# Values projected one head ahead in a two-layer attention and convolution trunk

## The chip, the cores and the metric

One core of a Trainium2 chip runs the whole program. The metric is device time in microseconds (us) for one execution; the kernel before takes 2388.18 us, the median of 3 runs between 2387.6 and 2389.5.

## The reference

The input is 1024 tokens of width 1024, ahead of which 16 learned tokens are set, so L = 1040. Two layers follow. Each normalises the rows (RMS norm), multiplies by `w_in`, and splits the product into queries, keys and values of 4 heads and a 1024-wide input of a convolution branch:

```python
proj = hn @ w_in[l]
q, k, v, u = jnp.split(proj, [QK_WIDTH, 2 * QK_WIDTH, 2 * QK_WIDTH + ATTN_WIDTH], axis=-1)
...
a = p[:, :, 0] - lam * p[:, :, 1]
return jnp.einsum('bhqk,bkhe->bqhe', a.astype(v.dtype), v)
```

A head has two causal softmaxes `p`, whose difference weights the values; each head's output is normalised. The convolution branch takes the halves `a` and `gate` of `u`, forms `a * sigmoid(gate)` (a gated linear unit, GLU), convolves it with 31 taps for each channel, normalises over channels and applies SiLU. Both branches go through `w_out` and are added to the residual; then comes a SwiGLU feed-forward net of width 2816. The last step is an RMS norm.

## The kernel before, in words

Activations lie transposed, 128 channels on the partitions and the 1040 tokens along the free axis. A product in float32 is made of three matmuls of split operands, `hi*hi + hi*lo + lo*hi` (`mm3`, L272), so a weight block of 1024 by 128 costs 24 matmuls per stretch of tokens. The stretches are CH0: 272, 384 and 384 columns. Weights come by `fetch`, which takes them in the fixed order of `plan`, prepares one key ahead (AHEAD = 1), and splits each half block on ScalarE (L222) and VectorE (L223). For the input projection the keys run 0 to 19: head h has keys 3h and 3h+1 for queries and keys and 3h+2 for values; keys 12 to 19 are the four GLU blocks.

A layer's mixing stage is written in this order. The norm's column factors come from `rsqrt_cols` (matmuls L177, a power on GpSimd, L183) and are spread over the partitions by `spread` (VectorE L198, TensorE L199, ScalarE L202). The first head's queries and keys are projected by `project_qk`; in the first layer its matmuls are those of L360, which take the token blocks as they arrive and hold three `pj` buffers of PSUM until ScalarE copies them out (L368). There are just three `pj` buffers. Then, for each head h: `make_stacks` lays out queries and keys by 12 DMAs (L399); `project_v` projects this head's values (matmuls L272, copy L428, transposes L413 and L417, scaled copies L414 and L420); the head before is finalized; and `weave` runs the attention (scores L455 and L456, mask L463, softmax on VectorE and ScalarE L460 to L471, transposes L483 and L492, values L503) with a filler between its steps: the next head's `project_qk`, for the third head also the first GLU block, for the fourth head GLU blocks 1 and 2. After the fourth head come GLU block 3, `finalize` (a power on GpSimd at L535), the convolutions of blocks 2 and 3 on TensorE (`conv`, with weights that VectorE makes at L610), and the output projection of the attention half (`wout_attn`).

The convolutions of blocks 0 and 1 are done on VectorE instead (`conv_dve`): one L588 and 30 L590 for each block, each over some 1040 columns and each needing the one before, then one ScalarE copy, L592. They can start when the block's GLU is done, whose last instruction is the VectorE product of L580. They are queued in `bg`; `tick` emits one for each 2300 ns that the steps claim, and `flush` emits those left after `wout_attn(1)`. Behind them stands `conv_norm`: matmuls L636 over all four blocks, squares, another `rsqrt_cols` and `spread`, SiLU (L648) and the split that the convolution half of the output projection needs. The rest of `wout_attn`, blocks 2 to 7, is woven into `conv_norm`.

What is written sets a priority, not the final order: a scheduler places the instructions of each engine ahead of the run and may put later ones earlier where their inputs and buffers are ready. On the chip an engine then keeps that order.

Of the kernel before, what the change touches and what calls it, by code (L numbers as in the profile page):

```python
# [23 lines left out]
NH = 4  # L24
# [17 lines left out]
LA = 2  # L42

PRODS = ("a11", "s3", "s2", "s1", "a12", "a22", "s4")
OCN = (0, 4, 1, 5, 2, 6, 3, 7)
RA = 2.0
DVEJ = (0, 1)
# [34 lines left out]
def tok(i):  # L82
    return (0, META) if i == 0 else (META + P * (i - 1), META + P * i)


def build(tc, xT, w_in, w_out, w_gu, w_down, params, lams, ctab, consts, tabs, outT):
# [14 lines left out]
    def nm(s):  # L101
        uid[0] += 1
        return f"{s}{uid[0]}"

    def big(dt=F32):
        return sp.tile([P, SW], dt, tag="S", name=nm("S"), bufs=SB)
# [11 lines left out]
    def tmp(dt=F32):  # L118
        return tp.tile([P, TW], dt, tag="T", name=nm("T"), bufs=TB)
# [15 lines left out]
    def small(n=NQ):  # L135
        return tp.tile([P, 16], F32, tag="small", name=nm("s"), bufs=16)

    def ps(tag):
        return pp.tile([P, 512], F32, tag=tag, name=nm(tag), bufs=PS_BUFS[tag])
# [29 lines left out]
    def rsqrt_cols(sq, n, blocks=range(NQ)):  # L169

        i0, i1 = blocks[0], blocks[-1] + 1
        pst = ps("sc")
        ms = small()
        V.memset(ms, 1.0)
        for i in blocks:
            a, b = tok(i)
            T_.matmul(pst[:b - a, i:i + 1], lhsT=sq[:, a:b], rhs=ones[:, 0:1], start=True, stop=True)  # L177
        f0 = max(i0, 1)
        V.tensor_scalar(ms[:, f0:i1], pst[:, f0:i1], 1.0 / n, EPS, op0=ALU.mult, op1=ALU.add)
        if i0 == 0:  # L180
            V.tensor_scalar(ms[:META, 0:1], pst[:META, 0:1], 1.0 / n, EPS, op0=ALU.mult, op1=ALU.add)
        rc = small()
        G.tensor_tensor(rc[:, i0:i1], ms[:, i0:i1], mhalf[:, i0:i1], op=ALU.pow)  # L183
        return rc

    def spread(rc, blocks=range(NQ), out=None):

        r = big() if out is None else out
        for k0, k1 in KCH:
            bl = [i for i in blocks if k0 <= tok(i)[0] < k1]  # L190
            if not bl:
                continue
            pb = ps("sc")
            dg = tmp()
            for i in bl:
                a, b = tok(i)
                n_ = b - a
                V.tensor_scalar(dg[:n_, a - k0:b - k0], ident[:n_, :n_], rc[:n_, i:i + 1], None, op0=ALU.mult)  # L198
                T_.matmul(pb[:, a - k0:b - k0], lhsT=ones[:n_, :], rhs=dg[:n_, a - k0:b - k0],  # L199
                          start=True, stop=True)  # L200
            lo, hi = tok(bl[0])[0], tok(bl[-1])[1]
            S.activation(r[:, lo:hi], pb[:, lo - k0:hi - k0], AF.Copy)  # L202
        return r
# [28 lines left out]

    def make_plan(sub_ts):
        for l in range(DEPTH):
            for b in range(20):
                plan.append((("in", l, b), (w_in[l, b], KD), False))
            for n in range(KD):
                plan.append((("oa", l, n), (w_out[l, n, :, 0:4, :], 4, sub_ts[l]), False))
            for n in OCN:
                plan.append((("oc", l, n), (w_out[l, n, :, 4:8, :], 4), False))  # L240
            f0 = 0
            for gi, gn in enumerate(GROUPS[l]):
                for n in range(KD):
                    end = l == DEPTH - 1 and gi == len(GROUPS[l]) - 1
                    plan.append((("dn", l, gi, n), (w_down[l, n, :, f0:f0 + gn, :], gn), end and n >= 4))
                f0 += gn
# [9 lines left out]
    def fetch(*key):  # L256
        i = [p[0] for p in plan].index(key)
        make(i)
        j = i + AHEAD
        if j < len(plan) and not (plan[j][0][0] == "dn" and plan[j][0][3] == 0):  # L260
            make(j)
        return made.pop(key)
# [4 lines left out]
    def mm3(out, w, xs, c0, c1):  # L267

        n = len(xs)
        for q, (wi, xi) in enumerate(((0, 0), (0, 1), (1, 0))):  # L270
            for k in range(n):
                T_.matmul(out, lhsT=w[k][wi], rhs=xs[k][xi][:, c0:c1],  # L272
                          start=(q == 0 and k == 0), stop=(q == 2 and k == n - 1))
# [24 lines left out]
    def tick(c):  # L298

        credit[0] += c  # L300
        while credit[0] >= BGSTEP:
            credit[0] -= BGSTEP
            if bg:
                bg.pop(0)()
# [5 lines left out]
    def weave(main, filler, ratio):  # L310
        tm = tf = 0.0
        for c in main:
            tm += c
            tick(c)
            while tf < tm * ratio:
                x = next(filler, None)
                if x is None:
                    break
                tick(x)
                tf += x  # L320

    def drain(*gens):
        for g in gens:
            for c in g:
                tick(c)

    def drain_n(g, n):
        for _ in range(n):
            tick(next(g, 0.0))
# [10 lines left out]
    def padded(which):  # L340
        turns[which] += 1
        return pads[which][turns[which] % 2]
# [61 lines left out]
    def project_v(l, h, rcol, out):  # L404
        wv = fetch("in", l, 3 * h + 2)
        v0 = padded(0)
        vv = big()
        out += [v0, vv]
        def turn(vT, c0, c1):
            s0 = max(c0, META)  # L410
            if c0 == 0:
                px = ps("tr")
                T_.transpose(px[:META, :P], vT[:, 0:META], ident)  # L413
                S.activation(v0[:META, :], px[:META, :P], AF.Copy, scale=rcol[:META, 0:1])  # L414
            px = ps("tr")
            for a in range(s0, c1, P):
                T_.transpose(px[:, a - s0:a - s0 + P], vT[:, a - c0:a - c0 + P], ident)  # L417
            for a in range(s0, c1, P):
                i = 1 + (a - META) // P
                S.activation(vv[:, a - META:a - META + P], px[:, a - s0:a - s0 + P], AF.Copy,  # L420
                             scale=rcol[:, i:i + 1])

        prev = None
        for c0, c1 in CH0:
            pv = ps("pj")
            mm3(pv[:, :c1 - c0], wv, hs, c0, c1)
            vT = tmp()
            S.activation(vT[:, :c1 - c0], pv[:, :c1 - c0], AF.Copy)  # L428
            if prev:
                turn(*prev)  # L430
            prev = (vT, c0, c1)
            yield 10 * (c1 - c0) + 300
        turn(*prev)
# [226 lines left out]
    nlams, subs = [], []  # L660
# [21 lines left out]
    for l in range(DEPTH):  # L682
# [10 lines left out]
        if l == 0:  # L693
# [15 lines left out]
                        tt(sqacc[:, c0:c1], sqacc[:, c0:c1], t, ALU.add)  # L709
            nc.sync.dma_start(con, consts)  # L710
        rcol = rsqrt_cols(sqacc, D)
        rs = spread(rcol)
        cosr, sinr = big(), big()
        for t, i in ((cosr, 0), (sinr, 1)):
# [16 lines left out]
        def glus(js):  # L731
            for j in js:
                yield from glu(l, j, rs, zs)
                if j in DVEJ:
                    conv_dve(l, j, zs[j][0], ys)

        st, vs = [], []
        drain(project_qk(l, 0, cosr, sinr, st, pre))
        if l == 0:
            for i in range(DEPTH):  # L740
# [1 line left out]
        cats, fin = [], []  # L742
        for h in range(NH):
            stacks = make_stacks(st)
            vs = []
            drain(project_v(l, h, rcol, vs))
            if fin:
                finalize(*fin.pop())
            st = []
            if h + 2 == NH:  # L750
                fill, ratio = chain(project_qk(l, h + 1, cosr, sinr, st), glus((0,))), RA
            elif h + 1 < NH:
                fill, ratio = project_qk(l, h + 1, cosr, sinr, st), 1.3
            else:
                fill, ratio = glus((1, 2)), 1.8
            weave(attention(l, h, stacks, *vs, nlams[l], cats, fin), fill, ratio)
            drain(fill)
        fill = glus((3,))
        drain_n(fill, 2)
        finalize(*fin.pop())  # L760
        weave(conv(l, 2, *zs[2], ys), fill, 2.4)
        drain(fill)
# [9 lines left out]
        fill = chain(wout_attn(0), wout_attn(1))  # L772
# [3 lines left out]
        fill = chain(*[wout_attn(n) for n in range(2, KD)])  # L776
# [8 lines left out]
        homes = hh + hl  # L785
        xc = {q: [None] * 4 for q in PRODS}

# [96 lines left out]

        steps = [(j, q) for j in range(NF) for q in PRODS]
        nprep = [0]
# [21 lines left out]
        def some(n):  # L908
            while n and todo:
                if next(todo[0], 0) == 0:  # L910
                    todo.pop(0)
                else:
                    n -= 1

        no = 0
        for i, n in enumerate(OCN):
            w = fetch("oc", l, n)
# [12 lines left out]
        some(99)  # L930
        todo += [squares(n) for n in OCN[4:]]

# [75 lines left out]
        for j in range(NF):  # L1008
# [3 lines left out]
                phase[1].tile([P, L], F32R, tag="m", name=nm("m"), bufs=4) for _ in range(2)]  # L1012
            for q in PRODS:
                ahead(i + LA)
# [174 lines left out]
```

## Time and profile before

| what | value |
|---|---|
| median of 3 runs | 2388.18 us (2387.6 to 2389.5) |
| the profiled execution | 2387.03 us |
| its span, first to last instruction | 2385.3 us |
| mean granted TensorE clock | 0.992 |
| TensorE busy | 2333.7 us, 98% |
| VectorE busy | 1670.9 us, 70% |
| ScalarE busy | 987.2 us, 41% |

The span is what the profile divides; the execution's own time holds some 2 us more around it. A busy share is an average over all stages. A row of instructions gives its time, and in brackets the idle time ahead of it with what ended that. PE is TensorE, DVE VectorE, ACT ScalarE, POOL GpSimd, SP the engine that issues DMAs.

### The profile page before, as it was taken

How to read it: one execution, taken by the hardware profiler on the slowest of the kernel's cores; microseconds unless marked ns; L12 is line 12 of the kernel's file. 1: busy time of each engine (PE TensorE's matmuls, PEld its weight loads, DVE VectorE, ACT ScalarE, POOL GpSimd, SP SyncE). 2: the span in 40 equal slices, each digit the busy share in tenths (PEclk: the TensorE clock that was granted, in tenths of full speed). 3: DMA queues.
4: the chain of work that ended last, by engine and by line, in shares of the span. 5: the costliest groups of instructions: out<-in, count | busy, mean ns of one | idle time of the engine just before them, and what ended most of it. 6: DMA issues, size and time to landing. Idle time of an engine off the chain costs nothing.

```text
span 2385.3 us, 36659 instructions
## 1 busy us (share of the span) xinstructions
PE 2333.7 (98%) x14407; PEld 2140.8 (90%) x14407; DVE 1670.9 (70%) x3476; ACT 987.2 (41%) x2074; POOL 33.8 (1%) x29
## 2 busy tenths in 40 slices
PE   8999999999999999999999999999999999999998
PEld 7899999989999999999999999987788888888887
DVE  7676799786656657566766768997856556556566
ACT  5565462553323223233535555536523223233242
POOL 0000000000000000000000000000000000000000
PEclk9999999999999999999999999999999999999999
DMA  4332422101112121111244314221121121111212
GB/s 163 94 76 68 121 66 61 49 29 60 46 45 64 35 63 40 59 56 43 90 128 102 74 44 112 76 54 45 36 62 55 43 62 39 59 59 39 60 56 71
DMA packets 84460, 155.29 MB, mean 65 GB/s; under 512 B 10048, under 2 KB 33600, under 8 KB 84288
## 3 DMA queue, kind: packets, MB, share of 16 engines
q1 hardware_dynamic: 84288, 152.95, 22.2%
q8 instruction: 114, 1.87, 0.3%
q14 instruction: 58, 0.48, 0.1%
HBM read 114.64 MB, written 8.45 MB: 52 GB/s over the span
## 4 chain that ended last, share of the span: by engine, by line
PE 86%; DVE 9%; ACT 2%; issue 1%; POOL 1%; DMA 1%; SPq 1%; DVEq 0%; POOLq 0%; ACTq 0%
PE pj L272 26%; PE sc L901 16%; PE pj L901 10%; PE tr L901 10%; PE sc L272 10%; DVE S L590 4%; PE tr L503 3%; PE tr L272 2%; PE sc L455 2%; PE tr L492 1%; PE sc L456 1%; PE sc L199 1%; DVE S L293 1%; DVE cw L610 1%; DVE S L286 1%
## 5 line engine op out<-in xcount | busy, mean ns | idle before, releaser
L272 PE MATMUL pj<-hh,w 128*128 128x384 f32 (+1 forms) x1776 | 342.5, 327 | 0.7 <-ACT S L368 0.7
L285 ACT ACTIVATE w<-w 128x512 fp32r<-128x512 f32 x308 | 187.0, 627 | 318.5 <-DVE w L293 242.9
L286 DVE TENSOR_TENSOR w<-w,w 128x512 fp32r<-128x512 f32 x308 | 209.5, 690 | 128.9 <-PE sc L901 53.8
L272 PE MATMUL pj<-S,w 128*128 128x384 f32 (+3 forms) x1164 | 296.2, 351 | 1.5 <-ACT S L285 0.9
L272 PEld LDWEIGHTS pj<-hh,w 128*128 128x128 f32 x1776 | 285.9, 189 | 2.7 <-ACT S L368 1.0
L901 PE MATMUL sc<-S,w 128*128 128x260 f32 (+1 forms) x1188 | 286.3, 322 | 0.0
L222 ACT ACTIVATE w<-w 128x512 fp32r<-128x512 f32 (+1 forms) x204 | 117.6, 577 | 308.3 <-DMA w<-in_w_down 167.9
L272 PEld LDWEIGHTS pj<-S,w 128*128 128x128 f32 x1164 | 204.4, 188 | 22.8 <-ACT S L285 1.9
L901 PEld LDWEIGHTS sc<-S,w 128*128 128x128 f32 x1188 | 198.6, 191 | 17.7
L272 PE MATMUL sc<-m,w 128*128 128x384 f32 (+3 forms) x804 | 211.5, 346 | 0.0
L272 PE MATMUL pj<-m,w 128*128 128x384 f32 (+3 forms) x804 | 211.4, 346 | 0.0
L901 PE MATMUL sc<-hh,w 128*128 128x260 f32 (+1 forms) x594 | 192.3, 324 | 6.9 <-ACT w L285 6.9
L901 PE MATMUL sc<-hl,w 128*128 128x260 f32 (+1 forms) x594 | 190.9, 321 | 0.0
L272 PE MATMUL pj<-hl,w 128*128 128x384 f32 (+1 forms) x888 | 174.4, 327 | 0.0
L223 DVE TENSOR_TENSOR w<-w,w 128x512 fp32r<-128x512 f32 (+1 forms) x204 | 127.1, 623 | 51.7 <-ACT w L222 45.2
L901 PE MATMUL tr<-S,w 128*128 128x260 f32 (+1 forms) x594 | 157.8, 320 | 3.1 <-ACT S L802 3.1
L901 PE MATMUL tr<-hl,w 128*128 128x260 f32 (+1 forms) x594 | 158.1, 320 | 0.0
L901 PE MATMUL pj<-S,w 128*128 128x260 f32 (+1 forms) x594 | 158.1, 320 | 0.0
L901 PE MATMUL pj<-hh,w 128*128 128x260 f32 (+1 forms) x594 | 157.7, 320 | 0.0
L272 PEld LDWEIGHTS sc<-m,w 128*128 128x128 f32 x804 | 143.1, 188 | 12.7
L272 PEld LDWEIGHTS pj<-m,w 128*128 128x128 f32 x804 | 143.1, 188 | 12.6
L590 DVE SCALAR_TENSOR_TENSOR S<-S,par,S 128x1037 f32<-128x1037 f32 (+15 forms) x120 | 153.2, 1278 | 0.6
(214 smaller groups left out, 4599.4 us busy)
## 6 DMA issues: line engine op xcount, KB each, us to landing
w<-in_w_gu SPq DMA_DIRECT2D x176, 256.0 KB, 3.0
S<-ST SPq DMA_DIRECT2D x96, 260.0 KB, 5.2
w<-in_w_in SPq DMA_DIRECT2D x80, 256.0 KB, 3.2
w<-in_w_down SPq DMA_DIRECT2D x96, 192.0 KB, 2.4
w<-in_w_out SPq DMA_DIRECT2D x32, 256.0 KB, 2.8
S<-in_xT SPq DMA_DIRECT2D x8, 520.0 KB, 7.3
w<-in_w_down SPq DMA_DIRECT2D x16, 256.0 KB, 2.7
S<-in_tabs SPq DMA_DIRECT2D x4, 520.0 KB, 5.4
```

The costliest lines, as they stand in the source:

```text
L199: T_.matmul(pb[:, a - k0:b - k0], lhsT=ones[:n_, :], rhs=dg[:n_, a - k0:b - k0], start=True, stop=True)
L222: S.activation(hi, rw, AF.Copy)
L223: V.tensor_tensor(lo, rw, hi.bitcast(F32), op=ALU.subtract)
L272: T_.matmul(out, lhsT=w[k][wi], rhs=xs[k][xi][:, c0:c1], start=(q == 0 and k == 0), stop=(q == 2 and k == n - 1))
L285: S.activation(hi, src, AF.Copy)
L286: V.tensor_tensor(lo, src, hi.bitcast(F32), op=ALU.subtract)
L293: V.tensor_tensor(o, a, b, op=op)
L455: T_.matmul(pc[:sz, :n], lhsT=qs[:, qa:qb], rhs=kk[:, k0:k1], start=True, stop=False)
L456: T_.matmul(pc[:sz, :n], lhsT=qs[:, qa:qb], rhs=kl[:, k0:k1], start=False, stop=True)
L503: T_.matmul(po[:sz, :P], lhsT=lh, rhs=rh, start=(j == 0), stop=(j == len(blocks) - 1))
L590: bg.append(lambda o=o: V.scalar_tensor_tensor(y[:, o:L], z[:, :L - o], cw(o), y[:, o:L], op0=ALU.mult, op1=ALU.add))
L901: T_.matmul(outs[c][:, :s1 - s0], lhsT=w[wi][:, k * P:(k + 1) * P], rhs=xc[q][k][xi][:, s0:s1], start=(first and p == 0 and k == 0), stop= ...
```

## The change

The values of head h+1 are projected ahead of head h's attention, so head 0 has two value projections in front of it, heads 1 and 2 one, and head 3 none. In front of head 3's scores stand two of the six steps of GLU block 1 instead, and the filler's ratio for that head goes from 1.8 to 1.6. In the first layer, the first stretch (272 columns) of head 0's values is written ahead of `spread`. Three steps of GLU block 3, not two, stand ahead of the last `finalize`. The order of `w_in`'s keys in the plan follows the new order of use.

```diff
+INS = (0, 1, 2, 5, 3, 4, 8, 6, 7, 11, 9, 10, 12, 13, 14, 15, 16, 17, 18, 19)
...
-            for b in range(20):
+            for b in INS:
...
         rcol = rsqrt_cols(sqacc, D)
+        vs = [[] for _ in range(NH)]
+        values_of = [project_v(l, h, rcol, vs[h]) for h in range(NH)]
+        if l == 0:
+            tick(next(values_of[0]))
         rs = spread(rcol)
...
-        st, vs = [], []
+        st = []
...
             stacks = make_stacks(st)
-            vs = []
-            drain(project_v(l, h, rcol, vs))
+            if h == 0:
+                drain(values_of[0])
+            if h + 1 < NH:
+                drain(values_of[h + 1])
             if fin:
                 finalize(*fin.pop())
...
             else:
-                fill, ratio = glus((1, 2)), 1.8
-            weave(attention(l, h, stacks, *vs, nlams[l], cats, fin), fill, ratio)
+                fill, ratio = glus((1, 2)), 1.6
+                drain_n(fill, 2)
+            weave(attention(l, h, stacks, *vs[h], nlams[l], cats, fin), fill, ratio)
             drain(fill)
         fill = glus((3,))
-        drain_n(fill, 2)
+        drain_n(fill, 3)
         finalize(*fin.pop())
```

## Rows read from the trace of the kernel before

**Rows 1.** The page, part 1: busy time, share of the span, instructions of each engine

```profile
PE 2333.7 (98%) x14407; PEld 2140.8 (90%) x14407; DVE 1670.9 (70%) x3476; ACT 987.2 (41%) x2074; POOL 33.8 (1%) x29
```

**Rows 2.** Windows: busy us of PE, PEld, DVE, ACT, POOL; granted clock, DMA share, GB/s

```profile
31.90:39.40 7.50, 4.31 (x18) 3.98 (x18) 3.47 (x14) 1.56 (x5) 1.80 (x1) 0.55 0.00 0
...
64.50:76.20 11.70, 6.88 (x31) 5.44 (x30) 4.47 (x27) 4.43 (x19) 0.00 (x0) 0.71 0.67 172
...
263.20:415.60 152.40, 149.28 (x1017) 143.04 (x1016) 146.12 (x279) 67.88 (x153) 5.47 (x2) 1.00 0.32 88
415.60:458.90 43.30, 41.37 (x246) 37.68 (x245) 32.03 (x64) 27.20 (x32) 1.80 (x1) 1.00 0.11 33
1443.90:1595.40 151.50, 147.69 (x968) 137.91 (x966) 144.76 (x267) 67.25 (x145) 5.47 (x2) 1.00 0.33 89
1595.40:1638.10 42.70, 40.06 (x183) 30.82 (x181) 29.47 (x56) 26.80 (x31) 2.15 (x1) 1.00 0.12 36
```

**Rows 3.** Timeline of TensorE, 61.5 to 73 us, head 0's first scores

```profile
64.36 0.17 PE L456 MATMUL sc<-S,S 128*16 128x16 f32 x1
65.93 0.55 PE L417 MATMUL tr<-con,T 128*128 128x128 f32 x3 [1.40 <-ACT S L420]
67.66 0.34 PE L455 MATMUL sc<-S,S 128*16 128x16 f32 x2 [1.18 <-DMA S<-ST]
...
70.46 0.49 PE L456 MATMUL sc<-S,S 128*16 128x16 f32 x2 [2.23 <-DMA S<-ST]
```

**Rows 4.** Chain that ended last, in DVE's and the tail's stretch: start us, us, what

```profile
263.82 0.63 DVE S L580
264.48 0.83 DVE S L588
265.34 1.31 DVE S L590
...
414.39 1.19 DVE S L590
415.61 2.15 ACT S L592
417.80 2.06 PE sc L636 x6
...
458.91 1.22 PE pj L272 x7
```

**Rows 5.** Chain, whole stretches of 24 matmuls, of 272 and of 384 columns

```profile
243.65 3.00 PE pj L272 x24
247.67 4.20 PE pj L272 x24
```

**Rows 6.** Timeline of TensorE, 28 to 40.2 us, around the norm's spreading

```profile
29.52 1.19 PE L177 MATMUL sc<-ones,S 128*16 128x1 f32 x10
30.56 0.55 PE L360 MATMUL tr<-hh,w 128*128 128x272 f32 x2
30.95 0.95 PE L177 MATMUL sc<-ones,S 128*128 128x1 f32 x8
34.42 4.31 PE L199 MATMUL sc<-T,ones 16*128 16x16 f32 x18 [2.52 <-DVE T L198]
39.45 0.65 PE L272 MATMUL pj<-hh,w 128*128 128x272 f32 x3 [0.72 <-ACT S L368]
```

**Rows 7.** Timeline of ScalarE, the value copies of head 3 in layer 0

```profile
264.76 0.39 ACT L428 ACTIVATE T<-pj 128x272 f32<-128x272 f32 x1
...
275.05 0.49 ACT L428 ACTIVATE T<-pj 128x384 f32<-128x384 f32 x1 [3.81 <-PE pj L272]
```

**Rows 8.** Groups of VectorE instructions in 263.2 to 415.6 us

```profile
L590 DVE SCALAR_TENSOR_TENSOR S<-S,par,S 128x1039 f32<-128x1039 f32 (+29 forms) x60 | 76.6, 1277 | 0.3
...
L293 DVE TENSOR_TENSOR ST<-pj,ST 128x384 f32<-128x384 f32 (+1 forms) x10 | 5.0, 507 | 0.0
...
L226 DVE SCALAR_TENSOR_TENSOR w<-w,subs,w 128x512 fp32r<-128x512 f32 x4 | 3.0, 746 | 0.0
```

**Rows 9.** Timeline of VectorE: a wait on finalize's power, head 2 of layer 0

```profile
272.33 0.17 DVE L293 TENSOR_TENSOR s<-s,s 128x9 f32<-128x9 f32 x1 [1.69 <-POOL s L535]
```

**Rows 10.** Timeline of SyncE: the 12 stack issues of head 0, then of head 3

```profile
52.63 13.17 SPq L399 DMA_DIRECT2D S<-ST  x12
...
260.25 13.32 SPq L399 DMA_DIRECT2D S<-ST  x12
```

**Rows 11.** The page, part 6: issues of the stacks, KB each, us to landing

```profile
S<-ST SPq DMA_DIRECT2D x96, 260.0 KB, 5.2
```

**Rows 12.** Waits of TensorE over the span: us in total, times, longest us

```profile
PE sc L456 <- DMA S<-ST: 2.2, 1, 2.2
...
PE sc L455 <- DMA S<-ST: 1.2, 1, 1.2
```

## The prediction

> **What bounds the kernel now.** I read the page's busy times first [rows 1]: TensorE is busy 98% of the span, VectorE 70%. Over the whole kernel only some 50 us are there for a better order to win, and this change touches the mixing stage of each layer alone. The windows by stage come next [rows 2]: the reader is to see two stretches in which TensorE stands. Around the norm's spreading it is busy 4.31 of 7.50 us at a granted clock of 0.55, around the first scores of the first layer 6.88 of 11.70 us at 0.71. The timeline says what it waits for in the second [rows 3]: 1.40, 1.18 and 2.23 us, for a value copy and for stacks that are still landing. Then I followed the chain that ended last through the end of the stage [rows 4]. It leaves TensorE at the end of GLU block 0, at 263.82, for the 30 + 30 steps of the two VectorE convolutions, goes from the last of them, at 414.39, through the copy L592 into the channel norm, and reaches the convolution half of the output projection near 458.9. So this stretch hangs on VectorE too. The windows agree [rows 2]: from 263.20 to 415.60 VectorE is busy 146.12 of 152.40 us, in layer 1 from 1443.90 to 1595.40 it is busy 144.76 of 151.50. It has 6.3 and 6.7 us left.
>
> **The change part by part.**
>
> *Values one head ahead, at head 0 of layer 0.* The second head's values now stand ahead of the first scores, work that needs no stack. One head's values cost one stretch of 272 columns and two of 384, 3.00 + 4.20 + 4.20 = 11.4 us [rows 5], and nine transposes; three took 0.55 us [rows 3], so nine take at most 1.6 and, as they overlap, I take 1.0: 12.4 us. That is more than the 4.81 us of waits. The bounds are 0 (the engine keeps the order the scheduler chose; if the stacks land later than it assumed, the work stands behind a waiting score) and 4.8; I take 4.0, since 12.4 us of free work is far over what is asked. The clock was granted at 0.71 over 11.70 us [rows 2], so 0.29 * 11.70 = 3.4 us of clock were withheld right after the engine had stood; with it fed, 0 to 3.4 come back, and I take half, 1.7, since part of that stretch was waiting and not streaming. Gain: 5.7 us, once.
>
> *The first stretch ahead of the spreading.* It takes 3.00 us [rows 5], and TensorE stood for 2.52 us there and 0.72 us behind it [rows 6]. But what did the first value matmuls wait for before? Not for their place: L177, written ahead of L360, stands among L360, so the scheduler fills holes as it finds them, and the values came in at 39.45, the moment that ScalarE had copied out a `pj` buffer (released by L368). All three `pj` buffers are held by the first head's queries and keys from the start, and the change gives no fourth. So I take 0. The best case is the two idles, 3.2 us, and the clock of that window, 0.45 * 7.50 = 3.4 us [rows 2]. The worst case is that the stretch now goes ahead of the rest of L360 when the buffer comes free, and the stacks start up to 3.0 us later, behind which the second head's values now stand as cover.
>
> *The price: GLU block 0 comes later.* The values of head 3 stood behind block 0, with copies from 264.76 to 275.05 [rows 7], just when VectorE had begun its convolutions at 265.34 [rows 4]. Now they stand in front of head 2's attention, and so in front of block 0, with the values of heads 1 and 2 likewise a head earlier. Block 0 is finished 12.4 us later, counted in TensorE's work, in each layer. From there VectorE has all its 146.12 and 144.76 us still to do; not one of its instructions belongs to the values. The two convolutions alone are 76.6 us [rows 8]. TensorE on the other hand has 12.4 us less from there: 149.28 - 12.4 = 136.9. VectorE becomes the longer of the two, and what it ends with, the channel norm, comes later by 12.4 less what it can make up. It can make up its idle time, 6.3 and 6.7 us, of which waits on finalize's power on GpSimd, 1.69 us at one of two finalizes [rows 9], stay (some 3 us for both); and it can put off what is not needed yet: 4 of the 10 additions of L293 at 507 ns that belong to later blocks of the output projection, 3 splits of L226 at 746 ns, together 4.3 us [rows 8], though these then fall into the norm. Behind it the tail from 415.60 to 458.90 leaves TensorE 43.30 - 41.37 = 1.9 us. Bounds of what is made up: 0 and 6.3 + 4.3 = 10.6 us. I take 5 for each layer: 3.5 of idle time and 1.5 of the rest. Loss: 12.4 - 5 = 7.4 us, in each of two layers.
>
> Here a rule speaks the other way. By the Trainium skill, Perfetto Trace Analysis, section "Identifying the Most-Contended Engine", the engine with the highest occupancy is the one to optimise, TensorE being judged by the busy share of its weight loads. Over the span that is TensorE, 90% of loads against VectorE's 70%, and by it the sum would be the gain alone, 5.7 us faster. Within the stretch that matters the same measure already puts VectorE first, 146.12 against 143.04 us of loads [rows 2], so I go by the stretch.
>
> *Head 3's scores behind two GLU steps.* The cover in front of them is 3.00 + 4.20 = 7.2 us, not 12.4. The 12 issues take 13.32 us on SyncE [rows 10] and the last lands some 5.2 us later [rows 11]. TensorE also has the end of head 2's attention and further GLU steps to take forward, and while it waits VectorE has its convolutions, so I take 0; 0 to 5.2 us for each layer. Nothing is queued on SyncE that was not before: the keys are reordered, not added.
>
> *The rest.* The ratio 1.6 and the third GLU step ahead of the last finalize move work within a stretch in which VectorE is the longer; 0, hidden by its chain. The values' ticks (11300 / 2300, some 5 steps) no longer emit convolution steps, so about 5 more stay for the flush; VectorE takes the chain up as soon as it is free in any case, as at 265.34, so 0. Heads 1 and 2 keep one projection of values as cover each.
>
> **Sum.** Layer 0: -5.7 + 7.4 = +1.7; layer 1, where no score waits for a stack (each of these waits is there once in the span [rows 12]), +7.4. Together +9.1 us on 2387.03 of the profiled execution, 2396.1. That execution lies 1.2 us below the median of the runs, so I predict 2397.
>
> **The rivals.**
> - *Faster: TensorE stays the bound.* If VectorE makes up all 12.4 us in each layer, by putting off work and by a shorter tail, the 5.7 us of gain stand alone: 2388.2 - 5.7 = 2382.5. For it: 98% against 70% [rows 1]. Against it: its bound of 10.6 us. It decides from 12.4 - 2.9 = 9.5 us made up in a layer. Chance 0.20.
> - *No change:* the gain at its upper end without the spreading, 8.2 us, and 8 us made up in each layer: 2 * 4.4 - 8.2 = +0.6, 2389. Chance 0.25.
> - *The first stretch does find a buffer,* contrary to my reading of the release: 3.2 us and half the clock, 1.7, less: 2392. Chance 0.10.
> - *Head 3 stands for its stacks,* 5 us in all, because GLU steps run out of `pj` buffers: 2402. Chance 0.10.
> - *My forecast,* 2397, about 2392 to 2402. Chance 0.35.
>
> About 0.2%, 4.8 us, is what a measurement of this kernel can tell from no change. Faster by more has rival 1 and little else: 0.21. Within it lie most of the second and half of the third rival: 0.27. Slower is the rest: 0.52. The range 2384 to 2406 leaves out the better half of the first rival, and a layer in which nothing is made up. The slower cases alone lie between 2393 and 2406.
>
> **What would show it.** Right: TensorE no longer waits for stacks at the first scores, and that window's clock is near 1.00; the last L580 of block 0 comes some 12 us later in layer 1 measured from that layer's start, and some 7 in layer 0; VectorE is busy over 97% from there to L592; TensorE waits more ahead of L636 or in the tail. Wrong: L592 comes at the old time or earlier from the layer's start, which means that VectorE had more to put off than I found; or TensorE's idle time at the spreading is gone.

## The result and the profile after

The changed kernel takes 2411.01 us (median of 5 runs, 2410.81 to 2412.78), the kernel before 2387.96 us in the runs beside it. The ratio is 1.0099, 95% interval 1.0087 to 1.0111: 23 us slower, outside the range that was given. The page's first part, against [rows 1]:

```profile
span 2410.7 us, 36676 instructions
...
PE 2337.2 (97%) x14407; PEld 2145.9 (89%) x14407; DVE 1672.5 (69%) x3476; ACT 987.6 (41%) x2076; POOL 32.9 (1%) x29
```

For the same count of instructions TensorE is busy 3.5 us more than before, VectorE 1.6 us more; so 21.9 of the 25.4 us that the span grew by are time in which TensorE stands. To see where, both traces are divided at the same events: the first issue of a head's stacks, the last VectorE convolution's copy, the first matmul of the feed-forward net. A row has the stretch, its length, the busy us of PE, PEld, DVE, ACT and POOL, TensorE's granted clock, and DMA. First the windows of the kernel before: to head 0's stacks, to head 1's, the first 40 us from head 3's stacks, from there to the copy of the second VectorE convolution, the tail up to the feed-forward net; then these last three for layer 1:

```profile
0.00:52.63 52.63, 42.19 (x238) 40.45 (x239) 39.62 (x77) 29.24 (x50) 2.64 (x9) 0.94 0.42 157
52.63:106.84 54.21, 49.39 (x311) 44.77 (x310) 35.31 (x139) 27.91 (x92) 0.00 (x0) 0.94 0.35 86
...
260.25:300.25 40.00, 38.64 (x261) 35.66 (x259) 34.62 (x93) 19.43 (x62) 2.76 (x1) 1.00 0.59 162
300.25:415.61 115.36, 113.59 (x779) 110.10 (x779) 112.61 (x189) 50.56 (x96) 2.71 (x1) 1.00 0.24 65
415.61:500.67 85.06, 83.13 (x511) 79.44 (x509) 70.17 (x130) 50.18 (x70) 1.80 (x1) 1.00 0.11 35
...
1441.02:1481.02 40.00, 38.69 (x261) 35.76 (x260) 35.30 (x84) 17.65 (x56) 2.76 (x1) 1.00 0.61 166
1481.02:1595.43 114.41, 111.92 (x730) 104.79 (x729) 110.67 (x187) 51.18 (x94) 2.71 (x1) 1.00 0.24 64
1595.43:1680.80 85.37, 82.73 (x368) 65.60 (x367) 67.82 (x116) 50.69 (x72) 2.15 (x1) 1.00 0.11 37
```

The same eight of the changed kernel:

```profile
0.00:56.03 56.03, 39.46 (x239) 37.96 (x240) 41.27 (x79) 31.21 (x54) 2.63 (x9) 1.00 0.44 156
56.03:116.24 60.21, 60.07 (x401) 56.38 (x400) 37.85 (x141) 33.19 (x109) 0.00 (x0) 1.00 0.35 88
...
268.51:308.51 40.00, 33.27 (x200) 30.37 (x199) 33.11 (x78) 17.44 (x44) 2.76 (x1) 0.87 0.57 157
308.51:431.26 122.75, 119.67 (x810) 115.84 (x809) 117.83 (x210) 51.78 (x105) 1.80 (x1) 0.99 0.24 63
431.26:512.65 81.39, 76.25 (x461) 72.69 (x459) 65.88 (x122) 47.28 (x66) 1.79 (x1) 0.98 0.09 30
...
1467.80:1507.80 40.00, 35.81 (x229) 33.34 (x228) 34.31 (x89) 17.16 (x43) 2.76 (x1) 0.96 0.59 160
1507.80:1627.15 119.35, 115.76 (x733) 106.36 (x732) 115.80 (x189) 49.64 (x97) 2.74 (x1) 1.00 0.24 65
1627.15:1708.06 80.91, 72.80 (x316) 57.42 (x315) 64.52 (x111) 47.18 (x67) 2.18 (x1) 0.96 0.10 30
```

Three things are to be seen. **At the front** TensorE loses 3.40 us up to head 0's stacks, but then stands for only 0.14 us of the next stretch, where it stood for 4.82, and its clock is 1.00 instead of 0.94. **At head 3** it is busy 5.4 us less in the same 40 us, at a clock of 0.87, in layer 1 2.9 us less at 0.96; here something new stands in the way. **Behind that** the way to the convolution's copy takes 7.39 and 4.94 us longer and the tail is only 3.67 and 4.46 us shorter, although the values of head 3, 12.4 us by my costing, are no longer in these three stretches. Together these take 244.14 us in layer 0 against 240.42, and 240.26 against 239.78 in layer 1. So the values' move, which should have taken 12.4 us out of them, cost 12.4 + 3.7 = 16.1 and 12.4 + 0.5 = 12.9 us: my term was 7.4 for each. These are single traces: two runs below (without the early stretch, and with it in another buffer) share the code from head 3's stacks on, and in their traces the three stretches take 242.5 and 239.0 us, which makes the price 14.5 and 11.6 us.

At the front the timeline of TensorE answers to [rows 6]:

```profile
16.02 0.92 PE L362 MATMUL tr<-hh,w 128*128 128x272 f32 x2 [16.02 <-ACT w L224]
...
24.45 0.77 PE L274 MATMUL pj<-hh,w 128*128 128x272 f32 x4
25.06 0.46 PE L362 MATMUL pj<-hh,w 128*128 128x272 f32 x2
...
35.60 0.39 PE L201 MATMUL sc<-T,ones 16*128 16x16 f32 x2 [0.55 <-DVE T L200]
```

TensorE begins at 16.02 us, not at 6.67, and with `tr` buffers; the first head's projection (now L362) touches no `pj` buffer until the early stretch of values (L274) has taken one at 24.45. It is not the stretch that waits for the buffer, as I had it, but the projection.

At head 3 the timeline of TensorE has three new waits:

```profile
281.16 0.23 PE L551 MATMUL tr<-con,o 16*128 16x16 f32 x1 [1.50 <-DVE o L550]
...
285.63 0.17 PE L458 MATMUL sc<-S,S 128*16 128x16 f32 x1
289.29 0.48 PE L551 MATMUL tr<-con,S 128*128 128x128 f32 x1 [3.48 <-ACT S L552]
291.41 1.27 PE L274 MATMUL pj<-hh,w 128*128 128x272 f32 x4 [1.65 <-DVE S L295]
```

The first is for the VectorE step of finalize (L550), which itself follows the power on GpSimd. The second is for a copy of finalize on ScalarE, and ScalarE at that time:

```profile
288.45 0.31 ACT L468 ACTIVATE p<-p,s 16x16 f32<-16x16 f32 x1 [11.28 <-DVE s L467]
288.67 0.18 ACT L468 ACTIVATION_READ_ACCUMULATOR p<-p,s 16x1 f32 x1
288.76 1.32 ACT L552 ACTIVATE S<-tr 128x400 f32<-128x400 f32 x3
```

It had stood for 11.28 us in front of the first exponential, L468, with the copies L552 behind it in its queue. And VectorE, on which that waits:

```profile
284.42 2.61 DVE L592 SCALAR_TENSOR_TENSOR S<-S,par,S 128x1034 f32<-128x1034 f32 x2
286.94 0.15 DVE L465 TENSOR_TENSOR p<-sc,con 16x16 f32<-16x16 f32 x1
287.06 1.29 DVE L592 SCALAR_TENSOR_TENSOR S<-S,par,S 128x1032 f32<-128x1032 f32 x1
288.27 0.15 DVE L467 TENSOR_REDUCE s<-p 16x1 f32<-16x16 f32 x1
288.39 2.62 DVE L592 SCALAR_TENSOR_TENSOR S<-S,par,S 128x1031 f32<-128x1031 f32 x2
290.93 1.36 DVE L295 TENSOR_TENSOR S<-pj,S 128x272 f32<-128x272 f32 x3
```

The two score steps, 0.15 us each, stand between convolution steps (now L592) of 1.28 us. The score was there at 285.80, so by my estimate this order makes some 2.3 of the 3.48 us (1.14 ahead of L465, 1.18 ahead of L467); before that ScalarE stood for the score itself. Between such steps stands also the evacuation of the GLU, L295, which frees TensorE's next `pj` buffer, the third wait. Before, the values of head 3 gave TensorE work there whose buffers ScalarE empties; a GLU step needs VectorE.

### The profile page after: what moved, and what is told of

Read it like the earlier page. It is cut to its first block, busy times and chain, and to the rows that moved or that the text cites. A ratio compares the mean times of both kernels' runs of the same rounds, so it can differ in the third digit from the quotient of the medians.

```text
span 2410.7 us, 36676 instructions
## 1 busy us (share of the span) xinstructions
PE 2337.2 (97%) x14407; PEld 2145.9 (89%) x14407; DVE 1672.5 (69%) x3476; ACT 987.6 (41%) x2076; POOL 32.9 (1%) x29
## 4 chain that ended last, share of the span: by engine, by line
PE 87%; DVE 7%; ACT 2%; DMA 1%; issue 1%; POOL 1%; SPq 1%; POOLq 0%; DVEq 0%; ACTq 0%
PE pj L274 28%; PE sc L910 16%; PE pj L910 10%; PE tr L910 10%; PE sc L274 10%; PE tr L505 3%; DVE S L592 3%; PE tr L274 2%; PE tr L494 1%; PE sc L457 1%; PE sc L458 1%; PE sc L619 1%; DVE S L295 1%; PE tr L362 1%; PE sc L201 1%
## 5 line engine op out<-in xcount | busy, mean ns | idle before, releaser
L274 PE MATMUL pj<-hh,w 128*128 128x384 f32 (+1 forms) x1776 | 346.9, 329 | 3.9 <-DVE S L295 3.9
L274 PE MATMUL pj<-S,w 128*128 128x384 f32 (+3 forms) x1164 | 301.1, 354 | 11.4 <-ACT S L287 8.4
L274 PEld LDWEIGHTS pj<-hh,w 128*128 128x128 f32 x1776 | 288.4, 190 | 7.3 <-DVE S L295 5.0
L274 PEld LDWEIGHTS pj<-S,w 128*128 128x128 f32 x1164 | 207.0, 190 | 34.2 <-ACT S L287 10.7
L274 PE MATMUL sc<-m,w 128*128 128x384 f32 (+3 forms) x804 | 211.6, 346 | 0.0
L274 PE MATMUL pj<-m,w 128*128 128x384 f32 (+3 forms) x804 | 211.5, 346 | 0.0
L274 PE MATMUL pj<-hl,w 128*128 128x384 f32 (+1 forms) x888 | 174.3, 328 | 0.0
L274 PEld LDWEIGHTS pj<-m,w 128*128 128x128 f32 x804 | 143.0, 188 | 13.0
L274 PEld LDWEIGHTS sc<-m,w 128*128 128x128 f32 x804 | 143.0, 188 | 12.8
L592 DVE SCALAR_TENSOR_TENSOR S<-S,par,S 128x1039 f32<-128x1039 f32 (+14 forms) x120 | 153.7, 1281 | 0.7
```

What stands on the lines that cost most here:

```text
L274: T_.matmul(out, lhsT=w[k][wi], rhs=xs[k][xi][:, c0:c1], start=(q == 0 and k == 0), stop=(q == 2 and k == n - 1))
L592: bg.append(lambda o=o: V.scalar_tensor_tensor(y[:, o:L], z[:, :L - o], cw(o), y[:, o:L], op0=ALU.mult, op1=ALU.add))
```

## The experiments

They ran beside the kernel before, whose median was 2387.22 to 2387.73 us in them. Two theories stood against each other: **A**, GLU block 0 and so VectorE's convolutions come 12.4 us too late and VectorE makes up nothing; **B**, the start of head 3 is jammed.

### The early stretch taken out

```diff
-        if l == 0:
-            tick(next(values_of[0]))
```

> The change without the first stretch of values ahead of the spreading in layer 0. In the changed kernel TensorE begins at 16.02 us instead of 6.67, and the first head's stacks are issued 3.40 us later (56.03 against 52.63). If pj buffers are handed out in written order, so that this stretch takes the first of three and the first head's queries and keys wait for it, TensorE begins near 6.7 us again, the stacks near 52.6, and the time falls by about 3.4 us, to 2407 to 2408. If the late begin comes from elsewhere (the new order of weight keys), nothing changes: 2411.

2408.56 us, ratio 1.0092 (1.0076 to 1.0107). TensorE begins at 6.81 us, and the first stacks are issued at 52.16. Head 3's are issued at 266.62, 6.4 us later than before with 12.4 us more work done: the gain of the values ahead is 6.0 us, and the early stretch on top of it costs 1.9 up to there (268.51). Such differences of single traces are good to some 3 us: two runs below, those of the kernel before with fewer convolution steps, share its front, and have head 3's stacks at 259.71 and 263.01 where it has them at 260.25. In the median the difference to the change, 2.5 us, lies within what the two can tell apart; the late begin is shown, its price in the whole less surely.

### Head 3's values in their own place

```diff
-            if h + 1 < NH:
+            if h < 2:
                 drain(values_of[h + 1])
+            elif h == 3:
+                drain(values_of[3])
```

> The change, but the values of head 3 are projected in front of head 3's attention as before; heads 1 and 2 stay one ahead, the early stretch and the two GLU steps stay. Theory A, VectorE: GLU block 0 and with it the VectorE convolutions come a whole value projection, 12.4 us, too late in each layer, and VectorE makes up nothing of it; then block 0 comes back by 12.4 us in each layer and the time falls by 20 to 25 us, to 2386 to 2391, less a few us if head 2's scores, now without cover, wait for their stacks (18.5 us from first issue to landing): up to 2396. Theory B, the start of head 3: TensorE stands there 3.48 and 1.65 us because ScalarE holds the copies of finalize (L552) behind the exponential of the first score, and its clock halves for 10.2 us; the two GLU steps in front are still there, so most of the loss stays: 2403 or more.

2392.93 us, ratio 1.0023 (1.0013 to 1.0032): 18 of the 23 us come back. The keys of the weights follow the order of use. Windows of this kernel, the 40 us from head 3's stacks in either layer:

```profile
259.26:299.26 40.00, 38.69 (x259) 36.27 (x258) 35.62 (x80) 19.54 (x56) 2.76 (x1) 1.00 0.60 162
1443.96:1483.96 40.00, 38.11 (x252) 36.90 (x251) 34.54 (x77) 15.71 (x46) 2.74 (x1) 0.96 0.60 166
```

TensorE is busy there as before, 38.69 against 38.64 us, although the two GLU steps are still in front. So these steps alone don't make the jam; with the value work back it is gone. The run does not part A from B, since it undoes both. It stays 5.7 us above the kernel before: by its trace 3.6 us more go by from layer 1's spreading to head 3's stacks, and 2.2 and 3.8 us more from there to the convolution's copy. What makes these, no run shows.

### The early stretch alone

```diff
+        vs0 = []
+        first = project_v(l, 0, rcol, vs0)
+        if l == 0:
+            tick(next(first))
         rs = spread(rcol)
...
-            vs = []
-            drain(project_v(l, h, rcol, vs))
+            vs = [] if h else vs0
+            drain(project_v(l, h, rcol, vs) if h else first)
```

> The kernel before with nothing but the first stretch of head 0's values ahead of the spreading in layer 0. If buffers are handed out in written order: TensorE begins near 16 us, the stacks of head 0 are issued 3 to 4 us later, and as nothing new covers them the time rises by 3 to 4 us, to 2391 to 2392. If the stretch merely fills the idle time at the spreading: 2383 to 2386.

2384.54 us, ratio 0.9987 (0.9978 to 0.9997): 2.7 to 3 us faster than before. TensorE begins at 15.86 and head 0's stacks are issued at 55.88, and still head 3's are issued at 256.58, 3.7 us earlier. Its windows at the two places of [rows 2], the second a little longer:

```profile
31.90:39.40 7.50, 6.95 (x52) 6.65 (x52) 2.61 (x12) 2.08 (x5) 1.80 (x1) 1.00 0.40 144
...
64.50:80.00 15.50, 15.50 (x97) 15.09 (x95) 7.86 (x28) 5.32 (x18) 0.00 (x0) 1.00 0.60 147
```

The holes are filled, and the clock is held at 1.00. My expectation had the late begin with the sign of a loss; it is none here. That the late begin shifted work into these holes would explain the gain; but with the stretch in another buffer (below) TensorE begins at 6.91, is busy in all of the same two windows, 7.50 and 15.50 us, and the time is the same. So the late begin is not what fills the holes.

### Without the GLU steps in front

```diff
-                fill, ratio = glus((1, 2)), 1.6
-                drain_n(fill, 2)
+                fill, ratio = glus((1, 2)), 1.8
...
-        drain_n(fill, 3)
+        drain_n(fill, 2)
```

> The change without what it does to GLU blocks 1 to 3: no two steps in front of head 3's scores, ratio 1.8, two steps ahead of the last finalize. Theory B, the jam at the start of head 3 comes from these steps: the time falls by 5 to 12 us, to 2399 to 2406, and TensorE no longer stands 3.48 us for L552. Theory A, VectorE started late: within 2 us of the change, 2409 to 2413, since VectorE has the same work from the same point on.

2408.93 us, ratio 1.0093 (1.0078 to 1.0108), 2.1 us below the change and at the edge of what theory A gave. TensorE still waits 3.48 us for L552. The steps and the ratio are a side matter.

### Half of VectorE's convolutions

```diff
-        for o in range(1, CW):
+        for o in range(1, 16):
```

> The kernel before with the two VectorE convolutions cut to 15 of their 30 accumulating steps in each block (the later taps are left out), 30 steps of 1.277 us, 38 us of VectorE less in each layer. It is the other half of the next run. If VectorE is co-bound in the kernel before, some us come back here already, 2370 to 2385; if TensorE alone bounds it, 2385 to 2388.

> The change with the same 15 steps of each block left out. Theory A, VectorE started late and cannot make it up: with 38 us less to do in each layer it can, and of the 23 us between the changed kernel and the one before little is left; this kernel stands -4 to +4 us from e5_half_taps_before (the early parts of the change were worth 3.0 us at head 1 of layer 0: stacks issued 9.4 us later with 12.4 us more work done). Theory B, the start of head 3 (no value work in front of it, ScalarE's copies behind the exponential): that start is as it was, and the difference stays 10 us or more.

The later taps are left out in both. The kernel before goes to 2385.61 us (0.9989, 0.9980 to 0.9999), the change to 2395.24 (1.0035, 1.0020 to 1.0049). In the kernel before, half of VectorE's chain is worth 2 us, in the change 15.8. The difference between the two falls from 23.1 to 9.6 us: between what the theories said. In the change without half the steps the 40 us at head 3 are as they were, 33.23 us busy, for the first 15 steps are still there. So the late stretches have the larger part, and the start of head 3 stays as a second one.

### One step left

```diff
-        for o in range(1, CW):
+        for o in range(1, 2):
```

> The kernel before with 1 of the 30 accumulating steps left in each VectorE convolution (29 left out). It is the other half of the next run. VectorE was not what bounded the kernel before (half the steps brought 2 us), so about as e5_half_taps_before: 2383 to 2388.

> The change with 29 of the 30 steps left out in each block. With half the steps left out the late part of the stage recovered, but the start of head 3 lost as much TensorE time as in the full change (12.4 against 12.5 us in the 40 us from the stacks' first issue in layer 0), since the first steps were still there. If the convolution steps that stand in VectorE's queue ahead of the first scores and of the GLU evacuations make that loss, it goes now, and this kernel stands -4 to +3 us from e9_one_tap_before. If the loss is that nothing but GLU steps covers the stacks of head 3, it stays: +5 to +10 us.

2377.98 us (0.9960, 0.9945 to 0.9975; the runs spread from 2375.3 to 2380.1) and 2383.39 (0.9982, 0.9972 to 0.9991): 5.4 us of difference are left, which is what was expected of the missing cover and not of VectorE's steps. The two intervals leave it between about 1 and 10 us, and the two profiled executions are only 0.7 us apart, 2378.2 and 2378.9. (The 12.4 and 12.5 us of the expectation are not in the windows, which have 6.8 and 6.7 us not busy; that the start lost about as much stays.) Head 3 of the change without the steps, in layers 0 and 1:

```profile
268.16:308.16 40.00, 35.99 (x228) 32.71 (x226) 20.48 (x82) 23.85 (x58) 1.79 (x1) 0.96 0.58 161
1448.80:1488.80 40.00, 37.22 (x250) 34.89 (x249) 21.36 (x85) 22.39 (x51) 1.79 (x1) 1.00 0.60 166
```

The kernel before without these steps is busy 39.94 and 39.99 us there. So of the loss at head 3, 5.4 and 2.9 us with all steps, 4.0 and 2.8 are left with VectorE half idle: most of it is the missing cover, not VectorE's queue. TensorE still stands for finalize, on which it did not wait there before:

```profile
279.99 0.23 PE L551 MATMUL tr<-con,o 16*128 16x16 f32 x1 [2.69 <-DVE o L550]
```

It stands another 1.29 us for L552; the wait for the GLU's evacuation is gone. So VectorE's convolutions stand behind some 18 of the 23 us, within the spread above, and the rest fits head 3's bare start.

### GLU block 0 first in head 2's filler

```diff
-                fill, ratio = chain(project_qk(l, h + 1, cosr, sinr, st), glus((0,))), RA
+                fill, ratio = chain(glus((0,)), project_qk(l, h + 1, cosr, sinr, st)), RA
```

The keys of the weights were put in the new order of use.

> e3_early_stretch_alone (values in their own head) with the order of head 2's filler turned round: GLU block 0 ahead of head 3's queries and keys, which moves the start of VectorE's convolutions forward by some 23 us (six stretches of projection, 2 * 11.4). Theory A: VectorE is co-bound from that start on, so 4 to 12 us come off 2384.5: 2373 to 2381. Rival: TensorE is the bound or head 3's stacks come late now; 2384 to 2390.

> The change with head 2's filler turned round in the same way. Values stay one head ahead and nothing stands in front of head 3 but the two GLU steps. Theory A: VectorE gets back more than the 12.4 us it lost, so most of the loss goes: 2386 to 2396. Theory B, head 3's start lacks the value work: 2403 or more.

The first is the early stretch alone with this edit, the second the change with it: 2390.64 us (1.0013, 1.0003 to 1.0022) and 2422.92 (1.0147, 1.0132 to 1.0162), both worse than what they came from. In the first, VectorE begins 36 us earlier than without it and nothing is won: in layer 0 the copy of the second convolution comes at 398.54 instead of 411.89, and the net's first matmul at 502.29 instead of 496.84. There VectorE's chain was not the bound. The second lies where theory B had it, but says little on A, because head 3's queries and keys now come last and its stacks go out at 280.94 us, 12.4 later than in the change.

That a head start for VectorE does not pay when head 3 starts later still is all that follows.

### Finalize's copies on VectorE

```diff
-            S.activation(cat[:, s0:k1], pc[:, s0 - k0:k1 - k0], AF.Copy)
+            V.tensor_scalar(cat[:, s0:k1], pc[:, s0 - k0:k1 - k0], 1.0, 0.0, op0=ALU.mult, op1=ALU.add)
```

> The change with finalize's three copies per head (L552) moved from ScalarE to VectorE, some 1.5 us more for VectorE per head. If TensorE's 3.48 us ahead of the third transposes of finalize is ScalarE keeping its order (L552 behind the first exponential, which waits 11.28 us), that wait goes and the clock holds better: 3 to 8 us off, 2403 to 2408. If VectorE's congestion is behind it either way, the copies wait there: within 3 us of 2411 or above.

2416.60 us, ratio 1.0121 (1.0106 to 1.0136). The wait moves to the other engine and grows:

```profile
292.01 0.45 PE L551 MATMUL tr<-con,S 128*128 128x128 f32 x1 [5.81 <-DVE S L552]
```

So the copies wait in VectorE's queue too, and ScalarE's order alone is not the cause. How much of the 5.81 us is VectorE's added work, no run shows.

### The early stretch in both layers

Against the early stretch alone:

```diff
-        if l == 0:
-            tick(next(first))
+        tick(next(first))
```

> e3_early_stretch_alone (2384.5) with the early stretch in layer 1 too, where TensorE stands 0.95 us at the spreading and the tokens of the norm are already there. If it fills that: 2383 to 2384.5. If the buffer that it takes delays the first head's queries and keys: 2385 to 2388.

2386.76 us, ratio 0.9993 (0.9984 to 1.0003): no gain over the stretch in layer 0 alone.

### The early stretch in another buffer

The early stretch alone, and the change, each with this edit:

```diff
-            pv = ps("pj")
+            pv = ps("sc" if l == h == c0 == 0 else "pj")
```

> e3_early_stretch_alone (2384.5) with the PSUM buffer of that one stretch taken from sc, the kind that the spreading uses, instead of pj. If TensorE's late begin (15.86 us there) comes from pj buffers being handed out in written order, it begins near 6.7 us again, the first stacks are issued up to 3.2 us earlier than there, and the time falls by 0 to 3 us more, to 2381 to 2384. If the begin stays near 16 us, the buffer order was not the reason, and the time stays at 2384 to 2385.

> The change with the same edit. If the buffer order is the reason: TensorE begins near 6.7 us, head 0's stacks are issued near 52.6 instead of 56.03, and some 3 us come off, 2407 to 2409; what VectorE costs later stays. If not: 2410 to 2412.

2384.87 us (0.9986, 0.9977 to 0.9996) and 2406.30 (1.0078, 1.0063 to 1.0093). The begin is back, here of the first:

```profile
6.91 1.23 PE L360 MATMUL pj<-hh,w 128*128 128x272 f32 x3 [6.91 <-ACT w L222]
...
32.61 1.25 PE L272 MATMUL sc<-hh,w 128*128 128x272 f32 x8
```

That settles the begin: `pj` buffers are handed out in written order, so a tile written early and filled late blocks those written behind it. The stacks came back only in part, against what was expected: head 0's are issued at 55.47 us in the first (55.88 with the `pj` buffer, 52.63 in the kernel before) and at 54.05 in the second (56.03); the stretch's own 3 us of matmuls still stand ahead of them. For the change the other buffer is worth 4.7 us; by itself the early stretch does as well with either. The version with the early stretch alone is some 3 us faster than the kernel before, and 26 us faster than the change.

## Why the prediction was wrong

**The direction and the main mechanism were right.** Values one head ahead filled the first scores' waits, and GLU block 0 came later: the changed kernel's chain has the last L582 at 1470.02 in layer 1, 12.2 us later than before counted from that layer's spreading (the spreading itself comes 14.55 us later), where I wrote some 12. In layer 0 it is 8.3 us later, where I wrote some 7. Another sign that I gave did not come: VectorE, over 97% busy from there to the copy by my forecast, is busy 149.29 of 158.50 and 148.95 of 156.50 us, 94% and 95%.

**The gain at the front was right in size, 6.0 against 5.7 us,** as the run without the early stretch shows it alone, but no closer than single traces tell, some 3 us. In it TensorE is busy 13.86 of the 15.50 us behind 64.50 at a clock of 1.00, where it was busy 10.68 at 0.78.

**The step that failed is "VectorE can make up 5 us".** It made up next to none: the price was 16.1 and 12.9 us, not 7.4, so I had 14.2 us too little in all (11.3 by the other two traces). From its first convolution step to the copy of the second VectorE did not need 5 us less; it took 7.4 and 5.0 us more, of which 3.8 and 4.1 are more work and 3.6 and 0.8 more standing. Two things were wrong in it. I let VectorE put off additions and splits that belong to the output projection. The groups in 272.8 to 431.3 us, against [rows 8], show the reverse:

```profile
L592 DVE SCALAR_TENSOR_TENSOR S<-S,par,S 128x1039 f32<-128x1039 f32 (+29 forms) x60 | 76.8, 1281 | 0.3
...
L295 DVE TENSOR_TENSOR ST<-pj,ST 128x384 f32<-128x384 f32 (+1 forms) x12 | 6.2, 518 | 0.5 <-PE pj L274 0.5
L228 DVE SCALAR_TENSOR_TENSOR w<-w,subs,w 128x512 fp32r<-128x512 f32 x8 | 6.0, 751 | 0.5 <-ACT w L227 0.5
```

Eight splits of L228 in place of 4, and 12 additions in place of 10; in layer 1 eight in place of 5, and 8 in place of 6. My reading, which no run tests by itself: TensorE, with less to do, took the output projection earlier, and so its VectorE work came ahead of the end of VectorE's chain. And I gave VectorE its idle time back, but it was no fuller: 117.83 of 122.75 us, 96%, where it had 112.61 of 115.36, and in the 40 us before 33.11 where it had 34.62.

**"Head 3's scores: I take 0" failed with it.** I argued that TensorE may stand there because VectorE has its convolutions meanwhile. But TensorE lost 5.4 and 2.9 us of work and some of its clock. Part of it is VectorE's queue, which keeps its order: the scores' short steps and the GLU's evacuations stood behind convolution steps. The larger part is the missing cover, 4.0 and 2.8 us with nearly all of these steps gone: with no values in front, TensorE comes to finalize and to the scores before their inputs are there. My rival that head 3 stands (0.10) named this place, and the GLU's buffers, but not what is waited for: of 6.6 us of waits in layer 0, 5.0 are for finalize and 1.65 for such a buffer, none for stacks.

**The early stretch: "I take 0" had the wrong work waiting.** I read the release by L368 as the stretch waiting for a buffer, which it did before; written earlier, it got the buffer first. Alone the early stretch takes some 3 us off, and on top of the values ahead it loses 1.9 up to head 3, less than single traces can tell. The buffer is the likely cause of that loss: in the other one head 3's stacks go out at 264.58, 3.9 us earlier than in the change and 2.0 earlier than with no early stretch. TensorE's wait at the spreading, whose end I had named as a sign of being wrong, went from 2.52 to 0.55 us.

**The accounting.** Front 6.0 gained, early stretch 1.9 lost, head 3 and VectorE 16.1 + 12.9 lost: +24.9, against the forecast +9.1. Between the layers 2.6 more are lost, 717.1 to 719.7 us between the first matmul of the net and the next spreading, behind the last layer 1.8 are won, and another 0.2 are won ahead of layer 1's head 3 (12.2 us more there, against the 12.4 costed): 25.5, against the 25.4 us by which the span grew, the rest rounding. The 2.6 us between the layers are scatter: the code there is the same, and over all traces it takes 714.8 to 719.9 us. Nothing made up in either layer, which I gave as the bound, would have been 2407 by my sum, just past the range's end of 2406 (in one layer 2402, inside the range, against what I wrote); VectorE's chain growing was not among the cases.

The rule of the Trainium skill that I weighed, Perfetto Trace Analysis, "Identifying the Most-Contended Engine", fits the kernel before, where half of VectorE's steps are worth 2 us and all but one of each block 9.7. For the change it does not point at what pays: there the same steps are worth 15.8 and 27.6 us, with VectorE at 69% over the span and TensorE's weight loads at 89%.

## What to carry to other kernels

Work that is moved ahead as cover leaves a hole where it stood: list the waits that it covered there, ask which engine empties what takes its place, and cost the hole with these waits and that engine's queue order, not with its idle time. When a bound moves to another engine, the engine that has become free may run ahead, and then the new bound can get more work before its deadline; count its instructions in the stretch. And look at who is written first for each kind of buffer: a tile that is written early and filled late keeps the others waiting.

## What the runs showed of the hardware

I had not expected that TensorE can begin 9.2 us later and lose nothing: with the early stretch alone its clock is 1.00 in the windows where it was 0.55 and 0.71 to 0.78 before, and it stands in them for 0.55 us in all. Standing is not all that goes with a low clock: with the stretch in the other buffer TensorE is busy 7.50 of the 7.50 us from 31.90, right behind the norm's sums (L177), and the clock is 0.77 there; the whole takes the same time. The other way round, in the wait of 3.48 us at head 3 the changed kernel's clock fell to the lower of its two levels and stayed there for 10.25 us, most of it work:

```profile
287.75:298.00 10.25, 7.06 (x30) 6.60 (x31) 9.27 (x20) 2.14 (x8) 0.00 (x0) 0.50 0.51 200
```

By the Trainium skill, TensorE: Matmul & The Clock Gate, Part 1, the clock is low after idling and activity releases it; the trace agrees, with 0.50 in and behind that wait. Eight matmuls of 272 columns took 2.01 us in that stretch, at 294.25, and 1.16 us at a clock of 1.00, at 60.27. A short wait thus cost more than its length.
